# The fourth of five matrix units keeps its result in the rows of the residual, its convolution input in the tile of its left operand, and 237 vector instructions take their factor of one from a column

## The chip, the cores and the metric

One core of a Trainium2 chip runs the kernel in one launch. The metric is the device time of one execution in microseconds, the median over the runs shown. The engines of the core that matter are TensorE (PE, with its weight loads as PEld), VectorE (DVE), ScalarE (ACT), GpSimd (POOL) and SyncE (SP), whose queue issues all the transfers.

## The reference

A decoder layer over 4096 rows of 1024 numbers, all in fp32, cut to its skeleton:

```python
h = layer_norm(x)
a_val, a_gate, a_z, b_u, b_v, b_z = split(h @ w_in, 6)          # 512 columns each
a = silu(layer_norm(causal_depthwise_conv(a_val * sigmoid(a_gate), width=31)))
y_a = a * silu(a_z)
v = layer_norm(gelu(b_v)); sv = per_head_lower_triangular(w_s) @ v (chunks of 128 rows) + b_s
y_b = gelu(b_u) * sv * silu(b_z)
h = layer_norm(ALPHA * h + concat(y_a, y_b) @ w_out)             # the fourth unit, then a norm
out = h + sigmoid(h @ w_ple_gate + b) * (p @ w_ple)
```

## The kernel before

The large products are cut into five units of one shape: 4096x1024 times 1024x1024. Units 0 to 2 are three parts of `h @ w_in`, unit 3 is `w_out`, unit 4 is `w_ple_gate`. A unit has 16 steps p, each of 256 rows (two tiles j of 128). A step is one `group`, a Strassen-like scheme of seven products of 512 x 512 blocks; each product is 12 matmuls with 512 columns (a left part `ahi`, `alo` and a right part `whi`, `wlo`, three combinations, four slices of the contraction), so that a step is 84 large matmuls. The banks of the products are `pa`, `pb`, `pd`, `pe`.

Around the six points `between(i)` of a group, generators put the background work into the program: left operands of the next step, the rows' normalisation, the next unit's weights and the convolution. A scheduler then sets the order on each engine, with its own estimate of times, and gives each tile a slot of its pool. The pool `big` has seven slots of 8 KB a partition. It holds in unit 3: `hr` (the residual rows), `z` (the result), `cz` (the convolution's output and the factor silu(a_z)), `y` (the left operand), and `bq` (quarters of the weights of unit 4 on their way through four subtractions, written to `twD`). A transfer into a slot waits until the tile that held it has been read for the last time. All transfers stand in the one queue of SP, in the order of the program; one that waits holds back all behind it.

Unit 3 at step p (`body_d`): it issues the load of `hr` of p+1 (`load_h`, L706); starts `y_rows(p+2)`, which turns the convolution's output on TensorE (L679, bank `tc`), copies it to `y` on ACT (L684), takes its statistics, normalises it on ACT (L693), scales and shifts it on POOL (L695, L696), and multiplies it by silu(a_z) on POOL (L698); runs the group, whose result goes to `z`; writes in the background of the next step the normalised `z` to `zT` (`z_out`, ACT L720, transfer L721); and issues at its end the loads of p+3 (`load_y`, L664 to L671). During p = 1 to 4 the four `bq` quarters pass as well (`combos`, loads L187, direct writes L190, and four POOL subtractions, each with its write, L192 to L201).

`ss` (L91) is the helper by which VectorE combines two SBUF tiles: the low parts of weights (`wlo`, 70 of 128x1024), `v<-v,sgb` (64), `zr<-zr,c` and `zr<-zr,sg` (32 each), and 39 others, 237 instructions in all. The convolution (L388 to L399) uses the same instruction with a column of weights as its factor, on one SBUF and one PSUM input.

Of the kernel before, what the change touches and what calls it, by code (L numbers as in the profile page):

```python
# [8 lines left out]
F32 = mybir.dt.float32  # L9
# [3 lines left out]
ADD, SUB, MUL = ALU.add, ALU.subtract, ALU.mult  # L13
# [3 lines left out]
P = 128  # L17
S = 4096
D = 1024
# [3 lines left out]
C = 512  # L23
CT = C // P
# [40 lines left out]
def hybrid_layer_kernel(  # L65
# [17 lines left out]
    nc = tc.nc  # L83
    dma = nc.sync.dma_start
    act = nc.scalar.activation
    tt = nc.vector.tensor_tensor
    ptt = nc.gpsimd.tensor_tensor
    stt = nc.vector.scalar_tensor_tensor
    ID = AF.Identity

    def ss(out, a, b, op):  # L91

        return stt(out, a, 1.0, b, op0=MUL, op1=op)  # L93

    const = ctx.enter_context(tc.tile_pool(name="const", bufs=1))
    dram = ctx.enter_context(tc.tile_pool(name="dram", bufs=1, space=DRAM))
# [6 lines left out]
    def big(shape, name, dt=F32):  # L103
        return pool.tile(shape, dt, tag="big", name=name, bufs=7)
# [10 lines left out]
    def sbank(name):  # L115
        return pbank("S", name, 2)
# [4 lines left out]
    def flat(t):  # L121
        return t.rearrange("p k x -> p (k x)")
# [2 lines left out]
    make_identity(nc, ident)  # L125
    nhalf = const.tile([P, 2], F32, name="nhalf")
    nc.gpsimd.memset(nhalf, -0.5)
    cw_sb = const.tile([P, CT, W31], F32, name="cw_sb")
    cs_sb = const.tile([P, CT, NE], F32, name="cs_sb")
    cb_sb = const.tile([P, CT], F32, name="cb_sb")  # L130
# [6 lines left out]
    cD = [dram.tile([CT, P, SB // P, 2, P // 2], F32, name=f"cD{b}") for b in range(NS)]  # L137
    uD = [dram.tile([4, P, C], F32, name=f"uD{b}") for b in range(NB)]
    ybD = [dram.tile([2, P, C], F32, name=f"ybD{p}") for p in range(NP)]
    azD = [dram.tile([2, P, C], F32, name=f"azD{p}") for p in range(NP)]  # L140
    twD = [None] + [dram.tile([7, P, 4, C], F32, name=f"twD{u}") for u in range(1, 5)]

    def pair(t):
        return t.rearrange("j p d -> p j d")
# [3 lines left out]
    def moments(halves, mv):  # L148
        st = pool.tile([P, 2, 6], F32, tag="st", name="st", bufs=4)
        for i, h in enumerate(halves):  # L150
            nc.vector.bn_stats(st[:, i, :], h)
        nc.vector.bn_aggr(mv, st[:, 0 : len(halves), :])

    def mvtile(n):
        t = pool.tile([P, 2, 2], F32, tag="mv", name="mv", bufs=6)
        return t[:, 0:n, :]

    def scale_bias(mv):

        n = mv.shape[1]  # L160
        nb = pool.tile([P, 2], F32, tag="nb", name="nb", bufs=6)
        nc.vector.tensor_scalar(mv[:, :, 1], mv[:, :, 1], EPS, None, op0=ADD)  # L162
        ptt(mv[:, :, 1], mv[:, :, 1], nhalf[:, 0:n], op=ALU.pow)  # L163
        for j in range(n):
            nc.gpsimd.tensor_scalar(
                nb[:, j : j + 1], mv[:, j, 0:1], mv[:, j, 1:2], -1.0, op0=MUL, op1=MUL
            )
        return nb
# [11 lines left out]
    def combos(u):  # L180


        for c in range(4):
            q = big([P, 4, C], "bq")
            for i in range(2):
                for j in range(2):
                    dma(q[:, 2 * i + j], wq[u, i, j][:, c])  # L187
            yield
            for n, k in ((1, 0), (2, 2), (3, 3)):
                dma(twD[u][ROW[n]][:, c], q[:, k])  # L190
            ptt(q[:, 0], q[:, 1], q[:, 0], op=SUB)
            dma(twD[u][ROW[5]][:, c], q[:, 0])  # L192
            yield
            ptt(q[:, 1], q[:, 3], q[:, 1], op=SUB)
            dma(twD[u][ROW[7]][:, c], q[:, 1])
            yield
            ptt(q[:, 3], q[:, 3], q[:, 0], op=SUB)
            dma(twD[u][ROW[6]][:, c], q[:, 3])
            yield
            ptt(q[:, 2], q[:, 2], q[:, 3], op=SUB)  # L200
            dma(twD[u][ROW[4]][:, c], q[:, 2])  # L201
            yield
# [126 lines left out]
    def group(L, W, add, to12, to22, between, scale=None):  # L329


        def plus(dst, ps, i):
            if add is None:
                act(dst, ps, ID)  # L334
            elif scale is None:
                tt(dst, ps, add[i], op=ADD)
            else:
                stt(dst, add[i], scale, ps, op0=MUL, op1=ADD)

        pb = pbank("B", "pb")  # L340
        pe = pbank("E", "pe")
        product(pb, 1, L, W, True)
        product(pe, 5, L, W, True)
        pa = pbank("A", "pa")
        plus(pa, pb, 0)
        s5 = utile([P, C], "s5")
        plus(s5, pe, 3)
        between(0)
        product(pb, 6, L, W, False)
        u2 = utile([P, C], "u2")  # L350
        plus(u2, pb, 1)
        between(1)
        product(pe, 3, L, W, False)
        anchor[:] = [tt(to12, pe, u2, op=ADD)]
        between(2)
        product(pb, 7, L, W, False)
        pd = pbank("D", "pd")
        plus(pd, pb, 2)
        anchor[:] = [tt(to22, pb, s5, op=ADD)]
        between(3)  # L360
        product(pa, 2, L, W, False)
        between(4)
        product(pd, 4, L, W, False)
        between(5)
        return pa, pd
# [56 lines left out]
    def broadcast(src, n, name, tile_of=big):  # L422
        t = tile_of([P, n, src.shape[-1]], name)
        for i in range(n):
            dma(t[:, i], src[i : i + 1, :].partition_broadcast(P))
        return t
# [139 lines left out]
    for h in range(2):  # L566
        half = wsf[64 * h : 64 * (h + 1)].rearrange("p n (i m) -> p n i m", i=2)
        nc.gpsimd.affine_select(
            out=half, in_=half, pattern=[[0, NH], [1, 2], [2, 64]], compare_op=ALU.is_ge,
# [87 lines left out]
    Y, CZ, H, cgb = {}, {}, {}, []  # L657

    def load_y(p):
        b, q = p // 4, p % 4  # L660
        while (b, CT - 1) not in convolved:
            bg_conv.step(1)
        cz = big([P, 2, 2, C], "cz")
        dma(  # L664
            flat(cz[:, 0]).rearrange("p (c x) -> p c x", c=CT),
            cD[b][:, :, 2 * q : 2 * q + 2].rearrange("c p j h m -> p c (j h m)"),
        )
        dma(cz[:, 1], pair(azD[p]))
        CZ[p] = cz
        Y[p] = big([P, 2, D], "y")  # L670
        dma(Y[p][:, :, C:], pair(ybD[p]))  # L671

    def y_rows(p):
        cz, y = CZ.pop(p), Y[p]
        cc = flat(cz[:, 0]).rearrange("p (c j x) -> p c j x", c=CT, j=2)
        for j in (1, 0):
            tp = sbank("tc")
            for ct in range(CT):
                nc.tensor.transpose(  # L679
                    out=tp[:, ct * P : (ct + 1) * P],  # L680
                    in_=cc[:, ct, j],
                    identity=ident,
                )
            act(y[:, j, 0:C], tp, ID)  # L684
        yield
        mv = mvtile(2)
        for j in (1, 0):
            moments([y[:, j, 0:C]], mv[:, j, :])
        nb = scale_bias(mv)
        yield  # L690
        for j in (1, 0):
            ya = y[:, j, 0:C]
            act(ya, ya, ID, scale=mv[:, j, 1:2], bias=nb[:, j : j + 1])  # L693
            yield
            ptt(ya, ya, cgb[0][:, 0], op=MUL)  # L695
            ptt(ya, ya, cgb[1][:, 0], op=ADD)  # L696
            act(ya, ya, AF.Silu)
            ptt(ya, ya, cz[:, 1, j], op=MUL)  # L698
            yield

    def left_y(p, L):
# [2 lines left out]
    def load_h(p):  # L704
        H[p] = big([P, 2, D], "hr")
        dma(H[p], pair(hT[p]))  # L706
# [4 lines left out]
    def z_out(p, z):  # L711
        mv = mvtile(2)
        for j in range(2):
            moments([z[:, j, 0:C], z[:, j, C:]], mv[:, j, :])
            yield
        nb = scale_bias(mv)
        yield
        yield
        for j in range(2):
            act(z[:, j], z[:, j], ID, scale=mv[:, j, 1:2], bias=nb[:, j : j + 1])  # L720
            dma(zT[p][j], z[:, j])  # L721
            yield

    def body_d(p, L, W, between):
        if p == 1:
            bg_w.add(combos(4))
        h = H.pop(p)
        if p + 1 < NP:
            load_h(p + 1)
        if p + 2 < NP:  # L730
            bg_x.add(y_rows(p + 2))
        if p + 2 >= NP:
            bg_x.add(z_rows(p + 2 - NP))
        z = big([P, 2, D], "z")
        pa, pd = group(
            L, W, [h[:, 0, 0:C], h[:, 0, C:], h[:, 1, 0:C], h[:, 1, C:]],
            z[:, 0, C:], z[:, 1, C:], between, scale=ALPHA,
        )
        for j, ps in ((0, pa), (1, pd)):
            act(z[:, j, 0:C], ps, ID)  # L740
        bg_post.drain()
        bg_post.add(z_out(p, z))
        if p + 3 < NP:
            load_y(p + 3)
        elif p + 3 == NP:
            pb_.append(broadcast(prow, 2, "prow"))
            load_z(0)
        elif p + 2 == NP:
            load_z(1)
# [3 lines left out]
    def load_z(p):  # L753
        Z[p] = big([P, 2, D], "zr")
        dma(Z[p], pair(zT[p]))

    def z_rows(p):
        for j in (1, 0):
            ptt(Z[p][:, j], Z[p][:, j], pb_[0][:, 0], op=MUL)
            ptt(Z[p][:, j], Z[p][:, j], pb_[0][:, 1], op=ADD)  # L760
            yield
# [131 lines left out]
```

## Time and profile before

| | |
|---|---|
| runs | 1897.29, 1895.17, 1889.53 us; median 1895.17 |
| profiled execution | 1896.8 us, span 1895.0 us, mean granted clock 0.984 |
| instructions | 24385 |
| PE busy | 1802.0 us, 95% of the span |
| DVE, ACT, POOL busy | 1405.1, 893.4, 1270.2 us |
| HBM traffic | 211.02 MB read, 150.99 MB written |

A busy share near 95% on PE says that all that can be won lies in PE's gaps, in the stretches at a lower granted clock behind them, and in nothing else as long as PE has the same matmuls to do. Gaps show in views by stretch; the page gives means.

### The profile page before, as it was taken

What the parts mean: (1) busy time and instruction counts of PE and PEld (TensorE: products, weight loads), DVE (VectorE), ACT (ScalarE), POOL (GpSimd) and SP (SyncE); (2) the same over time, 40 slices, a digit from 0 to 9 for tenths busy, and PEclk for the clock granted to TensorE, in tenths of its full rate; (3) what the DMA queues carried; (4) which work ended last, traced back from release to release, by engine and by line L of the source; (5) the groups of instructions that cost most, each with busy time, mean ns of one, the idle gap of its engine ahead of it and who ended that gap; (6) DMA issues with size and microseconds to landing.
All of it is one profiled execution on the core that took longest, in us unless ns stands there. A gap on an engine that the chain in (4) does not pass through costs nothing.

```text
span 1895.0 us, 24385 instructions
## 1 busy us (share of the span) xinstructions
PE 1802.0 (95%) x8322; PEld 1471.8 (78%) x8322; DVE 1405.1 (74%) x2176; ACT 893.4 (47%) x1438; POOL 1270.2 (67%) x1015
## 2 busy tenths in 40 slices
PE   5799999999999999999999798999999899999999
PEld 3687788877788887788888677787887688888887
DVE  8636887797787777989889976886568756655654
ACT  4655565565455555634445544455546322332222
POOL 2878987458786676588669567776677755655541
PEclk9899999999999999999999998999999999999999
DMA  6579776586734444899666856755446322222211
GB/s 240 193 233 352 254 231 214 182 297 210 239 112 148 138 160 150 304 353 328 211 200 222 308 192 228 250 186 191 168 167 236 119 101 78 89 90 95 100 55 52
DMA packets 184940, 363.62 MB, mean 192 GB/s; under 512 B 49648, under 2 KB 74224, under 8 KB 177136
## 3 DMA queue, kind: packets, MB, share of 16 engines
q1 hardware_dynamic: 184816, 362.07, 55.4%
q8 instruction: 66, 1.08, 0.2%
q14 instruction: 58, 0.48, 0.1%
HBM read 211.02 MB, written 150.99 MB: 191 GB/s over the span
## 4 chain that ended last, share of the span: by engine, by line
PE 75%; DVE 10%; DMA 7%; ACT 3%; issue 3%; POOL 2%; SPq 0%; DVEq 0%; POOLq 0%; ACTq 0%
PE pb L316 9%; PE pb L317 9%; PE pb L318 9%; PE pe L318 6%; PE pe L316 6%; PE pe L317 6%; PE pp L809 5%; PE tp L261 3%; PE pd L316 3%; PE pd L317 3%; PE pd L318 3%; PE pa L316 3%; PE pa L317 3%; PE pa L318 3%; DVE wlo L93 2%
## 5 line engine op out<-in xcount | busy, mean ns | idle before, releaser
L236 POOL TENSOR_TENSOR alo<-s,ahi 128x512 fp32r<-128x512 f32 x192 | 266.7, 1402 | 275.5 <-ACT ahi L235 271.6
L316 PE MATMUL pb<-whi,ahi 128*128 128x512 f32 x960 | 386.8, 403 | 13.2 <-ACT pa L334 5.4
L317 PE MATMUL pb<-wlo,ahi 128*128 128x512 f32 x960 | 379.3, 395 | 1.9 <-DVE wlo L93 1.9
L318 PE MATMUL pb<-whi,alo 128*128 128x512 f32 x960 | 379.0, 395 | 0.1
L316 PE MATMUL pe<-whi,ahi 128*128 128x512 f32 x640 | 257.0, 402 | 16.8 <-ACT ahi L235 7.5
L317 PE MATMUL pe<-wlo,ahi 128*128 128x512 f32 x640 | 253.3, 396 | 4.2 <-DVE wlo L93 4.0
L318 PE MATMUL pe<-whi,alo 128*128 128x512 f32 x640 | 255.5, 399 | 1.6 <-POOL alo L236 1.5
L316 PEld LDWEIGHTS pb<-whi,ahi 128*128 128x128 f32 x960 | 183.1, 191 | 57.0 <-ACT pa L334 9.0
L318 PEld LDWEIGHTS pb<-whi,alo 128*128 128x128 f32 x960 | 182.7, 190 | 40.0 <-POOL alo L236 0.5
L317 PEld LDWEIGHTS pb<-wlo,ahi 128*128 128x128 f32 x960 | 183.2, 191 | 38.8 <-DVE wlo L93 2.9
L236 POOL TENSOR_TENSOR alo<-qa,ahi 128x512 fp32r<-128x512 f32 x128 | 171.5, 1355 | 44.9 <-ACT ahi L235 44.8
L390 DVE SCALAR_TENSOR_TENSOR acc<-ca,cs_sb,acc 128x512 f32<-128x512 f32 x240 | 180.0, 750 | 4.1
L235 ACT ACTIVATE ahi<-s 128x512 fp32r<-128x512 f32 x192 | 119.9, 629 | 131.6 <-DVE s L288 49.7
L399 DVE SCALAR_TENSOR_TENSOR acc<-ca,cw_sb,acc 128x512 f32<-128x512 f32 x240 | 179.1, 746 | 0.8 <-POOL ca L383 0.6
L396 DVE SCALAR_TENSOR_TENSOR acc<-zy,cw_sb,acc 128x512 f32<-128x512 f32 x224 | 167.0, 746 | 2.6 <-POOL zy L382 1.5
L316 PEld LDWEIGHTS pe<-whi,ahi 128*128 128x128 f32 x640 | 121.8, 190 | 42.2 <-ACT ahi L235 8.7
L236 POOL TENSOR_TENSOR alo<-qb,ahi 128x512 fp32r<-128x512 f32 x96 | 126.9, 1328 | 39.6 <-ACT ahi L235 38.8
L317 PEld LDWEIGHTS pe<-wlo,ahi 128*128 128x128 f32 x640 | 121.7, 190 | 30.3 <-DVE wlo L93 6.5
L236 DVE TENSOR_TENSOR alo<-tp,ahi 128x512 fp32r<-128x512 f32 x144 | 97.9, 684 | 62.1 <-ACT ahi L235 60.0
L318 PEld LDWEIGHTS pe<-whi,alo 128*128 128x128 f32 x640 | 121.7, 190 | 26.8 <-POOL alo L236 2.5
L316 PE MATMUL pd<-whi,ahi 128*128 128x512 f32 x320 | 129.9, 406 | 5.5 <-ACT pd L334 3.8
L163 POOL TENSOR_TENSOR mv<-mv,nhalf 128x2 f32<-128x2 f32 (+1 forms) x81 | 55.4, 690 | 108.6 <-DVE mv L162 108.0
(147 smaller groups left out, 3994.7 us busy)
## 6 DMA issues: line engine op xcount, KB each, us to landing
qa<-qD SPq DMA_DIRECT2D x32, 1024.0 KB, 6.2
twD<-bq SPq DMA_DIRECT2D x112, 256.0 KB, 5.8
wst<-twD SPq DMA_DIRECT2D x28, 1024.0 KB, 7.2
qb<-qD SPq DMA_DIRECT2D x32, 768.0 KB, 6.5
xr<-in_x SPq DMA_DIRECT2D x32, 512.0 KB, 5.6
hT<-xr SPq DMA_DIRECT2D x32, 512.0 KB, 3.8
qD<-s SPq DMA_DIRECT2D x64, 256.0 KB, 2.9
bq<-in_wq SPq DMA_DIRECT2D x64, 256.0 KB, 5.0
```

The costliest lines, as they stand in the source:

```text
L93: return stt(out, a, 1.0, b, op0=MUL, op1=op)
L163: ptt(mv[:, :, 1], mv[:, :, 1], nhalf[:, 0:n], op=ALU.pow)
L235: act(hi, src, ID)
L236: eng.tensor_tensor(lo, src, hi.bitcast(F32), op=SUB)
L261: nc.tensor.transpose(out=tp[:, kk * P : (kk + 1) * P], in_=rows[:, j, k * P : (k + 1) * P], identity=ident,)
L316: nc.tensor.matmul(ps, lhsT=ah[:, k, :], rhs=wh[:, k, :], start=start and k == 0, stop=False, **kw)
L317: nc.tensor.matmul(ps, lhsT=ah[:, k, :], rhs=wl[:, k, :], start=False, stop=False, **kw)
L318: nc.tensor.matmul(ps, lhsT=al[:, k, :], rhs=wh[:, k, :], start=False, stop=k == 3, **kw)
L390: stt(even, src, w, even, op0=MUL, op1=ADD)
L396: stt(dst, src, cw_sb[:, ct, 2 * k + 1 : 2 * k + 2], odd if k else even, op0=MUL, op1=ADD)
L399: stt(src if k == NE - 1 else even, src, cw_sb[:, ct, 2 * k : 2 * k + 1], even, op0=MUL, op1=ADD,)
L809: nc.tensor.matmul(pp, lhsT=l[:, k, ts], rhs=r[:, k, cs], start=k == 0 and l is ph and r is wp_hi, stop=k == 1 and l is pl,)
```

## The change

It has two parts. In unit 3 the result is written over the residual rows (`z = h`), and the convolution's output is loaded into the left half of `y`, in two transfers of 256 KB with pieces of 512 bytes where there was one of 512 KB with pieces of 1 KB; TensorE turns it out of `y` and ACT writes it back to the same place. `cz` then holds silu(a_z) alone, at half its size. A step so takes three slots of `big` (`hr`, `y`, `cz`) where it took four. In `ss`, the factor 1.0 is read from a column of ones in SBUF, and one POOL instruction fills this column.

```diff
     def ss(out, a, b, op):
-        return stt(out, a, 1.0, b, op0=MUL, op1=op)
+        return stt(out, a, one, b, op0=MUL, op1=op)
...
+    one = const.tile([P, 1], F32, name="one")
+    nc.gpsimd.memset(one, 1.0)
...
-        cz = big([P, 2, 2, C], "cz")
-        dma(
-            flat(cz[:, 0]).rearrange("p (c x) -> p c x", c=CT),
-            cD[b][:, :, 2 * q : 2 * q + 2].rearrange("c p j h m -> p c (j h m)"),
-        )
-        dma(cz[:, 1], pair(azD[p]))
-        CZ[p] = cz
         Y[p] = big([P, 2, D], "y")
+        for j in (1, 0):
+            dma(
+                Y[p][:, j, 0:C].rearrange("p (c x) -> p c x", c=CT),
+                cD[b][:, :, 2 * q + j].rearrange("c p h m -> p c (h m)"),
+            )
+        CZ[p] = big([P, 2, C], "cz")
+        dma(CZ[p], pair(azD[p]))
         dma(Y[p][:, :, C:], pair(ybD[p]))
...
-        cc = flat(cz[:, 0]).rearrange("p (c j x) -> p c j x", c=CT, j=2)
...
-                    in_=cc[:, ct, j],
+                    in_=y[:, j, ct * P : (ct + 1) * P],
...
-            ptt(ya, ya, cz[:, 1, j], op=MUL)
+            ptt(ya, ya, cz[:, j], op=MUL)
...
-        z = big([P, 2, D], "z")
+        z = h
```

The change also lets the scheduler order anew. On SP's queue, this is the stretch around the loads for step 4 of unit 3 (`cz_10539` before, `y_10543` after; `bq_10363` and `bq_10532` before, `bq_10367` and `bq_10536` after, are the first and second quarter; `z_10091` before and `hr_10086` after hold the result of step 0). Before:

```order
L201 DMA twD4_176<-bq_10363 128x512
L721 DMA zT0_93<-z_10091 128x1024
L187 DMA bq_10532<-in_wq 128x512
L721 DMA zT0_93<-z_10091 128x1024
L187 DMA bq_10532<-in_wq 128x512 x3
L190 DMA twD4_176<-bq_10532 128x512
L664 DMA cz_10539<-cD1_130 128x4x256
L668 DMA cz_10539<-azD4_161 128x2x512
L190 DMA twD4_176<-bq_10532 128x512
```

After:

```order
L203 DMA twD4_178<-bq_10367 128x512
L189 DMA bq_10536<-in_wq 128x512 x4
L192 DMA twD4_178<-bq_10536 128x512
L722 DMA zT0_95<-hr_10086 128x1024
L192 DMA twD4_178<-bq_10536 128x512
L722 DMA zT0_95<-hr_10086 128x1024
L192 DMA twD4_178<-bq_10536 128x512
L194 DMA twD4_178<-bq_10536 128x512
L667 DMA y_10543<-cD1_132 128x4x128 x2
```

The two writes of the result now stand behind the second quarter's loads and its first write, and the load for step 4 stands behind one write of `twD` that follows a POOL subtraction. In the slots, `y_10543` lies where `hr_10086` lay, so its load waits for both writes of `zT0`; `cz_10539` waited for them too.

The same queue around the loads for step 5 (`z_10299` before and `hr_10094` after hold the result of step 1; `bq_10762` and `bq_10766` are the third quarter). Before:

```order
L190 DMA twD4_176<-bq_10762 128x512
L721 DMA zT1_94<-z_10299 128x1024
L190 DMA twD4_176<-bq_10762 128x512 x2
L721 DMA zT1_94<-z_10299 128x1024
L664 DMA cz_10786<-cD1_130 128x4x256
L668 DMA cz_10786<-azD5_162 128x2x512
L192 DMA twD4_176<-bq_10762 128x512
L671 DMA y_10789<-ybD5_146 128x2x512
L706 DMA hr_10791<-hT4_81 128x2x1024
L195 DMA twD4_176<-bq_10762 128x512
```

After:

```order
L192 DMA twD4_178<-bq_10766 128x512 x3
L722 DMA zT1_96<-hr_10094 128x1024
L194 DMA twD4_178<-bq_10766 128x512
L722 DMA zT1_96<-hr_10094 128x1024
L197 DMA twD4_178<-bq_10766 128x512
L667 DMA y_10790<-cD1_132 128x4x128 x2
L672 DMA cz_10793<-azD5_164 128x2x512
L673 DMA y_10790<-ybD5_148 128x2x512
L200 DMA twD4_178<-bq_10766 128x512
```

The load for step 5 moved behind the writes of the first two POOL subtractions of the quarter (L194, L197), which stood behind it before (L192, L195). Its slot was that of a left operand (`y_10295`) and is now that of `hr_10094`, so it waits for `zT1` to be written, which it did not do before.

## Rows read from the trace of the kernel before

**Rows 1.** The page, busy time of each engine.

```profile
PE 1802.0 (95%) x8322; PEld 1471.8 (78%) x8322; DVE 1405.1 (74%) x2176; ACT 893.4 (47%) x1438; POOL 1270.2 (67%) x1015
```

**Rows 2.** The page, the chain that ended last, by engine.

```profile
PE 75%; DVE 10%; DMA 7%; ACT 3%; issue 3%; POOL 2%; SPq 0%; DVEq 0%; POOLq 0%; ACTq 0%
```

**Rows 3.** Windows: start and boundary to unit 4; length, PE, PEld, DVE, ACT, POOL, clock, DMA.

```profile
0.00:73.00 73.00, 38.39 (x130) 27.60 (x131) 62.61 (x83) 38.62 (x50) 32.44 (x31) 0.88 0.62 222
...
1456.00:1519.00 63.00, 54.41 (x231) 43.34 (x230) 48.82 (x53) 28.88 (x41) 45.10 (x24) 0.92 0.44 157
```

**Rows 4.** Windows, the first five steps of unit 3, same columns.

```profile
1078.00:1110.60 32.60, 24.30 (x111) 19.81 (x110) 26.45 (x36) 14.81 (x23) 20.59 (x17) 0.84 0.70 228
1110.60:1132.70 22.10, 21.76 (x106) 17.66 (x105) 18.55 (x35) 10.74 (x17) 16.79 (x19) 1.00 0.53 187
1132.70:1161.00 28.30, 25.35 (x114) 20.53 (x113) 16.77 (x32) 11.64 (x19) 17.36 (x18) 0.88 0.67 239
1161.00:1188.60 27.60, 23.57 (x109) 19.24 (x108) 20.32 (x39) 11.02 (x17) 22.83 (x23) 0.94 0.68 226
1188.60:1212.40 23.80, 22.36 (x109) 18.07 (x108) 18.26 (x35) 12.01 (x20) 18.34 (x20) 1.00 0.87 308
```

**Rows 5.** Waits ahead of the tile `tc`: releaser, us in all, times.

```profile
  DMA cz<-cD: 10.9, 6
  DVE alo L236: 6.4, 1
```

**Rows 6.** Timeline of PE in unit 3: start, us each, idle before and releaser.

```profile
1089.89 1.09 PE L679 MATMUL tc<-ident,cz 128*128 128x128 f32 x4 [6.37 <-DVE alo L236]
...
1139.45 1.09 PE L679 MATMUL tc<-ident,cz 128*128 128x128 f32 x4 [2.95 <-DMA cz<-cD]
...
1141.19 0.63 PE L318 MATMUL pb<-whi,alo 128*128 128x512 f32 x1
...
1168.34 1.11 PE L679 MATMUL tc<-ident,cz 128*128 128x128 f32 x8 [4.03 <-DMA cz<-cD]
```

**Rows 7.** Timeline of SP's queue before steps 4 and 5: start and length of an issue.

```profile
1127.93 0.41 SPq L721 DMA_DIRECT2D zT<-z  x1
...
1131.17 0.33 SPq L190 DMA_DIRECT2D twD<-bq  x1
1132.42 0.38 SPq L664 DMA_DIRECT2D cz<-cD  x1
...
1134.80 0.33 SPq L190 DMA_DIRECT2D twD<-bq  x1
...
1160.31 0.71 SPq L721 DMA_DIRECT2D zT<-z  x1
1161.11 1.10 SPq L664 DMA_DIRECT2D cz<-cD  x1
...
1168.61 0.33 SPq L195 DMA_DIRECT2D twD<-bq  x1
```

**Rows 8.** The page, transfers: count, KB each, median us from issue to landing.

```profile
zT<-z SPq DMA_DIRECT2D x32, 512.0 KB, 2.9
...
cz<-cD SPq DMA_DIRECT2D x16, 512.0 KB, 4.3
...
pf<-in_pT SPq DMA_DIRECT2D x16, 256.0 KB, 2.6
```

**Rows 9.** VectorE's groups by form: count | busy us, mean ns.

```profile
L390 DVE SCALAR_TENSOR_TENSOR acc<-ca,cs_sb,acc 128x512 f32<-128x512 f32 x240 | 180.0, 750 | 4.1
...
L93 DVE SCALAR_TENSOR_TENSOR wlo<-wst,whi 128x1024 fp32r<-128x1024 f32 x70 | 106.9, 1544 | 7.2 <-ACT whi L176 6.3 <-PE pb L318 0.8
...
L93 DVE SCALAR_TENSOR_TENSOR zr<-zr,c 128x512 f32<-128x512 f32 x32 | 43.9, 1373 | 1.0
...
L338 DVE SCALAR_TENSOR_TENSOR pa<-hr,pb 128x512 f32<-128x512 f32 x16 | 11.1, 694 | 13.1 <-PE pb L318 13.1
```

**Rows 10.** Instructions of line 93: count, ns min/median/max, first and last start.

```profile
L93 DVE SCALAR_TENSOR_TENSOR wlo<-wst,whi x70: 1164/1218/3379, 13.7 to 1475.4; 128x1024 fp32r<-128x1024 f32 x70
```

## The prediction

> **What bounds the kernel now.** I began with the busy times. PE is busy for 95% of the span [rows 1], and the chain that ended last lies on PE for 75%, on DVE for 10% and on transfers for 7% [rows 2]. The change takes no matmul away, so what it can win is PE's idle time and the time that PE runs at its lower clock. The windows show where these are. The first 73 us hold 34.6 us of idle time (73.00 - 38.39), and the passage to unit 4 holds 8.6 us in 63 [rows 3]. The rest that concerns the change lies in the first steps of unit 3: an undisturbed step takes 22.10 us at a clock of 1.00, and the first, third, fourth and fifth of these windows take 32.60, 28.30, 27.60 and 23.80 us [rows 4]. That is 10.5 + 6.2 + 5.5 + 1.7 = 23.9 us more. This stage is what the first part of the change works on.
>
> Next I asked what ends the idle time there. Ahead of the transposes into `tc`, PE waits 10.9 us for the load of the convolution's output and 6.4 us for `alo` on DVE [rows 5]. The timeline gives the single waits: 6.37 us in the first window, for DVE; 2.95 us in the third and 4.03 us in the fourth, both for the load [rows 6]. After each such gap a 512-column matmul takes 0.63 us [rows 6], and the window's granted clock falls to 0.84, 0.88 and 0.94 [rows 4]: parts of these windows run at 1.2 GHz, not 2.4. PE's busy time shows what this costs: 24.30, 25.35 and 23.57 us against 21.76, so 2.5, 3.6 and 1.8 us [rows 4].
>
> **The first gap.** The 6.37 us of the first window end with `alo` on DVE [rows 6]. DVE reaches it late, behind the split of the weights, and its order there hardly differs after the change. The transposed data are not what is late. I take 0 us for it, and its 10.5 us stay.
>
> **The loads for steps 4 and 5.** One fewer tile for each step should let loads go out earlier, but the slots and the queue decide. For step 4, PE was ready at 1139.45 - 2.95 = 1136.5. The load was issued at 1132.42 and its data came at 1139.45 [rows 6, 7], so it took 7.0 us, though the median for this kind of load is 4.3 [rows 8]. After the change the load still waits for both writes of the result of step 0, which now stand behind the second quarter's loads and its direct writes. The bounds: if the second write of `zT` still goes out at 1127.93 [rows 7], it lands 2.9 us later, at 1130.8, and a 256 KB load needs 2.6 us (the row of `pf`) [rows 8]; its data are there at 1133.4 and there is no wait. If this write goes out behind the quarter's second direct write, at 1134.80 + 0.33 [rows 7], it lands at 1138.0, and the load comes 2.6 to 4.3 us behind, at 1140.6 to 1142.3: a wait of 4.1 to 5.8 us. The quarter's loads no longer stand behind a write of `zT` that waits for ACT, so its chain starts earlier than before; I take the middle of the outer ends, 1137.9, a wait of 1.4 us, and 1.5 us less than before.
>
> For step 5, PE was ready at 1168.34 - 4.03 = 1164.3, the load was issued at 1161.11 and took 7.2 us [rows 6, 7]. Its new slot makes it wait for the result of step 1 to be written: with the second write issued at 1160.31 as before [rows 7] plus 2.9 us, the load goes out at 1163.2, later than before. But it now comes in halves of 256 KB, of which PE needs only the first to begin. It lands 2.6 to 4.3 us later, at 1165.8 to 1167.5, a wait of 1.5 to 3.2 us. The late end is the queue: the load stands behind the write of the quarter's second subtraction, which went out at 1168.61 before [rows 7]. If it does so again, the data come at 1171.5 to 1173.2, a wait of 7.2 to 8.9 us. On POOL the two subtractions now stand ahead of the left operands' subtractions that delayed them, so the early end is nearer. I take 1167, a wait of 2.7 us, and 1.3 us less.
>
> From step 6 on I take 0 us for the loads: only 1.7 us are to be had at one step, and thereafter the loads have a step in hand. The two shorter gaps take about half of one and a third of the other's time at the lower clock with them: 3.6 x 1.5 / 2.95 + 1.8 x 1.3 / 4.03 = 2.4 us, of which I count 1.5, since how long the clock stays low need not follow the length of the gap. The first part then gives -1.5 - 1.3 - 1.5 = -4.3 us. The 16 more transfers cost SP some 0.4 us each (the issue at 1132.42 took 0.38 [rows 7]), spread over 16 steps of 22 us. Writing the transposed values back into `y` adds no instruction.
>
> **The column of ones.** All 237 instructions of `ss` change their form. The trace has no instruction with two SBUF inputs and a column as factor. The nearest row is the convolution's: 750 ns with a column, on one SBUF and one PSUM input, against 694 ns for the same kind with a constant factor [rows 9]. So I take 56 ns more, and 237 x 0.056 = 13.3 us of DVE. Of DVE's 1405.1 busy us, the chain holds 10% of 1895.0, or 189.5 us, which is 13.5% [rows 1, 2]. By this share the path gets 1.8 us. The ends are 0 (all hidden behind PE) and 13.3 us (all on the path).
>
> Could the column make them faster? The splits `wlo` have a median of 1218 ns, a mean of 1544 and a maximum of 3379 [rows 10, 9], and `zr<-zr,c` has a mean of 1373 where the alone-standing form takes about 694 [rows 9]. The long ones lie beside POOL instructions. The Trainium skill, SBUF — State Buffer, "Who interferes with whom", says that a DVE instruction with two SBUF inputs contends with a GpSimd instruction that reads SBUF; the trace agrees (1373 ns against 694). Nothing in that rule depends on where the scalar comes from, and by "Scalar operands" of DVE: scalar operands, raw-bit mode, write accounting and state across instructions, a column takes up no second tensor stream; the second input of these instructions is still a tensor, so by both the stretch stays as it is. I take no gain here.
>
> **The order anew.** At the start and at the passage to unit 4 the scheduler puts DVE's splits and PE's pieces in a slightly other order. This work decides PE's idle 34.6 and 8.6 us [rows 3]. I take 0, with the 8.6 us of the passage as a bound to either side.
>
> **Sum.** 1896.8 - 4.3 + 1.8 = 1894.3 us. The profiled execution lies 1.6 us above the median of the runs, whose ends are 8 us apart; 0.5%, or 9.5 us, is about what a measurement of this kernel can tell from no change. I predict 1894 us.
>
> **Rivals.**
> - *The loads come early.* One fewer slot for each step puts all the waits for the convolution's output aside: 10.9 us [rows 5] and the 3.6 + 1.8 us of low clock, 16.3 in all, less 1.8 for the column: 1882 us. For it: seven slots for three tiles a step. Against it: slots that the writes of `zT` free late.
> - *The column frees DVE from GpSimd.* The stretched part of the two costliest groups goes: 70 x (1544 - 1218) ns = 22.8 us and 32 x (1373 - 694) ns = 21.7 us, 44.5 us of DVE [rows 9, 10], 13.5% of it on the path, 6.0 us. With it the backlog ahead of `alo` in unit 3 (6.4 + 2.5 us) and about half the passage's 8.6 us: 19 us together, so 1877 us. For it: the convolution's instructions with a column have a mean of 750 ns beside the same POOL. Against it: these have only one SBUF tensor.
> - *The loads come later (slower).* Both loads take their late ends, since the writes of a quarter of weights stand ahead of them: the waits become about 5.0 and 8.0 us instead of 2.95 and 4.03, +6.0, and the low clock grows with them by 3.6 x 2.1 / 2.95 + 1.8 x 4.0 / 4.03 = 4.3; with the column's 1.8, +12 and 1909 us. It decides from the point at which the write of the second subtraction for step 5 goes out after 1165 on before's clock.
> - *The form with a column reads its two tensors in turn.* Then each takes twice its 694 ns, 237 x 0.694 = 164 us of DVE and 13.5% of it on the path: 1919 us. Nothing in the trace speaks for it or shows that it is not so.
>
> **Chances.** Little change as summed: 0.47, its own range 1887 to 1903. Loads early: 0.15. Column frees DVE: 0.10. Loads later: 0.14. Tensors in turn: 0.03. Order anew beyond the bound: 0.06 faster, 0.05 slower. So faster 0.31, same 0.47, slower 0.22. From 1876 to 1910 the range takes in the first rival, most of the second and half or more of the third, and leaves out less than 2 in 10.
>
> **What would show it.** In unit 3 the waits of PE ahead of `tc` at steps 4 and 5 should be 1 to 3 us each, ended by the load into `y`, and the one of about 6 us behind `alo` should stand. The `v<-v,sgb` and `wlo` instructions should read some 50 ns longer where alone, and as stretched as before beside POOL. Wrong would be: medians of `zr<-zr,c` at 700 to 750 ns (the second rival); no waits for loads in unit 3 and a clock of 1.00 from the third window on (the first); waits of 5 us and more at steps 4 and 5 with `twD` writes ahead on SP's queue (the third); or a start longer or shorter by more than 9 us, which is the order alone.

## The result

The changed kernel is slower: 1911.31 us (median of 4 runs, 1908.88 to 1915.45) against 1896.23 us for the kernel before (4 runs, 1889.53 to 1898.48). The ratio is 1.0089, with a 95% interval from 1.0071 to 1.0107, that is 15 us or 0.9%. The forecast was 1894 us, from 1876 to 1910, with the largest chance on no change.

| us | before | changed |
|---|---|---|
| span of the profiled execution | 1895.0 | 1907.6 |
| PE busy | 1802.0 | 1805.4 |
| DVE busy | 1405.1 | 1420.7 |
| to the second step of unit 0 | 73.4 | 78.2 |
| from there to the first step of unit 3 | 1004.6 | 1003.9 |
| first five steps of unit 3 | 134.3 | 129.7 |
| its further ten steps | 221.6 | 221.9 |
| last step of unit 3 and six of unit 4 | 192.9 | 205.2 |
| the rest | 268.2 | 268.7 |

The stretches are taken between the first matmuls into `pb` of the steps. Two pieces lose, 4.8 us at the start and 12.3 us at the passage to unit 4; one gains, 4.6 us in the first steps of unit 3. The page of the changed kernel, busy time and then the chain by engine, answers to [rows 1, 2]:

```profile
PE 1805.4 (95%) x8322; PEld 1472.7 (77%) x8322; DVE 1420.7 (74%) x2176; ACT 893.7 (47%) x1438; POOL 1262.8 (66%) x1016
...
PE 76%; DVE 11%; DMA 5%; POOL 4%; issue 3%; ACT 1%; SPq 0%; POOLq 0%; DVEq 0%; ACTq 0%
```

DVE holds 15.6 us more, transfers have a smaller share of the chain, DVE and POOL a larger one. The windows of the changed kernel, for the start, the five steps, and 63 us from the first step of unit 4 (columns as in [rows 3, 4]):

```profile
0.00:73.00 73.00, 33.85 (x109) 23.57 (x110) 60.45 (x74) 35.17 (x44) 28.06 (x30) 0.86 0.57 202
1082.10:1114.00 31.90, 23.60 (x100) 18.75 (x101) 25.34 (x33) 15.01 (x24) 19.37 (x15) 0.84 0.64 214
1114.00:1136.60 22.60, 21.18 (x105) 17.16 (x104) 19.25 (x37) 9.74 (x16) 16.50 (x19) 1.00 0.62 215
1136.60:1159.70 23.10, 22.29 (x110) 18.10 (x109) 17.79 (x34) 10.20 (x16) 14.66 (x16) 1.00 0.77 260
1159.70:1186.00 26.30, 23.02 (x109) 17.95 (x108) 19.59 (x35) 12.66 (x20) 24.75 (x24) 1.00 0.76 261
1186.00:1211.90 25.90, 24.35 (x120) 19.99 (x119) 21.39 (x39) 10.71 (x17) 21.83 (x22) 1.00 0.84 269
1460.60:1523.60 63.00, 53.20 (x226) 41.72 (x225) 50.38 (x55) 27.11 (x39) 39.36 (x21) 0.92 0.38 132
```

The third of the five steps fell from 28.30 to 23.10 us and its clock rose from 0.88 to 1.00; the fourth fell by 1.3 us, its clock also at 1.00; the fifth grew by 2.1 us. The first, which waits for DVE, is nearly as long as before. The waits of PE in the changed kernel (releaser, us in all, times, longest):

```profile
PE tp L263 <- DVE xr L93: 22.2, 4, 11.4
...
PE pb L318 <- ACT pa L336: 8.1, 6, 3.9
PE pb L318 <- DVE pa L338: 7.1, 2, 3.6
...
PE pe L320 <- POOL alo L238: 3.9, 3, 3.1
...
PE tc L680 <- DMA y<-cD: 1.6, 1, 1.6
```

The same waits for `pa` in the kernel before:

```profile
PE pb L316 <- ACT pa L334: 5.4, 8, 1.5
...
PE pb L316 <- DVE pa L336: 2.4, 1, 2.4
```

The wait for the convolution's output, 10.9 us in [rows 5], is down to 1.6 us, and waits on the other engines have grown. One of them is in the fourth of these steps: PE waits 3.06 us for `alo` on POOL, where it had waited 4.03 us for the load.

```profile
1166.43 0.50 PE L320 MATMUL pe<-whi,alo 128*128 128x512 f32 x1 [3.06 <-POOL alo L238]
```

The instructions with the column in the changed kernel (count, ns min/median/max, first and last start; [rows 10] has the first of them before):

```profile
L93 DVE SCALAR_TENSOR_TENSOR wlo<-wst,one,whi x70: 1224/1274/3372, 13.7 to 1472.7; 128x1024 fp32r<-128x1024 f32 x70
...
L93 DVE SCALAR_TENSOR_TENSOR zr<-zr,one,c x32: 750/1254/1905, 1496.8 to 1898.4; 128x512 f32<-128x512 f32 x32
L93 DVE SCALAR_TENSOR_TENSOR zr<-zr,one,sg x32: 750/752/2158, 1508.7 to 1904.0; 128x512 f32<-128x512 f32 x32
```

They are 56 ns longer in the median of the splits (1218 to 1274), and the long ones beside POOL are still there. A split is the subtraction that makes the low part `wlo` of a weight.

### The profile page after: what moved, and what is told of

Its sections match the earlier page's. It is cut to its first block, busy times and chain, and to the rows that moved or that the text cites. A ratio compares the mean times of both kernels' runs of the same rounds, so it can differ in the third digit from the quotient of the medians.

```text
span 1907.6 us, 24493 instructions
## 1 busy us (share of the span) xinstructions
PE 1805.4 (95%) x8322; PEld 1472.7 (77%) x8322; DVE 1420.7 (74%) x2176; ACT 893.7 (47%) x1438; POOL 1262.8 (66%) x1016
## 4 chain that ended last, share of the span: by engine, by line
PE 76%; DVE 11%; DMA 5%; POOL 4%; issue 3%; ACT 1%; SPq 0%; POOLq 0%; DVEq 0%; ACTq 0%
PE pb L318 9%; PE pb L320 9%; PE pb L319 9%; PE pe L318 6%; PE pe L320 6%; PE pe L319 6%; PE pp L810 4%; PE tp L263 3%; PE pd L318 3%; DVE wlo L93 3%; PE pa L318 3%; PE pa L319 3%; PE pd L319 3%; PE pd L320 3%; PE pa L320 3%
## 5 line engine op out<-in xcount | busy, mean ns | idle before, releaser
L238 POOL TENSOR_TENSOR alo<-s,ahi 128x512 fp32r<-128x512 f32 x192 | 261.0, 1370 | 278.4 <-ACT ahi L237 267.0
L320 PE MATMUL pa<-whi,alo 128*128 128x512 f32 x320 | 127.8, 400 | 2.5 <-DVE alo L238 2.5
```

The source lines that it names most:

```text
L238: eng.tensor_tensor(lo, src, hi.bitcast(F32), op=SUB)
L320: nc.tensor.matmul(ps, lhsT=al[:, k, :], rhs=wh[:, k, :], start=False, stop=k == 3, **kw)
```

## The experiments

All were timed in five rounds against the kernel before on the same chip. The medians of before were 1891.12, 1892.96 and 1893.82 us in the three sets, so the ratios are compared, not the medians. Each ratio stands with its 95% interval.

**The column alone, the first part alone, and the halves of the first part.** The edits to the kernel before, in this order: the column; both edits of unit 3; the shared result; the load into `y`.

```diff
-        return stt(out, a, 1.0, b, op0=MUL, op1=op)
+        return stt(out, a, one, b, op0=MUL, op1=op)      # e1
...
-        z = big([P, 2, D], "z")
+        z = h                                            # e2, e3
...
+                Y[p][:, j, 0:C].rearrange("p (c x) -> p c x", c=CT),
+                cD[b][:, :, 2 * q + j].rearrange("c p h m -> p c (h m)"),   # e2, e4
...
```

> The kernel before with the column of ones alone. Theory A (the column is the loss: some 60 ns more for each of 237 instructions, at the start and the unit boundaries on the path, and an order made for it): +8 to +15 us, start about 5 us longer, the passage to unit 4 about 8 us longer. Theory B (the slots of the first part are the loss, at the passage to unit 4): 0 to +5 us, from the start alone. Theory C (each build gets its own order, and losses at the boundaries are its chance): anything from -5 to +15, not additive with the next run.

> The changed kernel with the constant 1.0 in place of the column, so the first part of the change alone. Theory A: faster than before by 4 to 9 us, since the waits for loads in steps 4 and 5 of unit 3 are gone. Theory B: slower by 5 to 10 us, with the loss at the passage to unit 4 still there. Theory C: not the difference of the changed kernel and the run with the column alone; its own sum of boundary waits.

> The kernel before with the result written over the residual rows alone (convolution output still loaded into cz). Theory A: -2 to -6 us: a slot more is free, the loads for steps 4 and 5 come earlier. Theory B: if this part is the loss at the passage to unit 4, +5 to +10 us. If the loads come no earlier, 0.

> The kernel before with the convolution output loaded into y in two halves and turned in place alone (result still in its own tile). Theory A: 0 to -4 us: the first half lands sooner, cz is half as large but holds a slot as before. Theory B: 0, if the loss needs the slot that the shared result frees.

Measured: the column alone 1.0083 (1.0070 to 1.0095); the first part alone 1.0015 (1.0006 to 1.0023); the shared result alone 1.0023 (1.0010 to 1.0037); the load into `y` alone 1.0054 (1.0042 to 1.0066). By the total, the column alone costs nearly what both parts cost, as theory A said. The places do not agree: theory A's 8 us at the passage to unit 4 are not in e1, whose seven steps there take 191.0 us where the kernel before takes 192.9 and the changed kernel 205.2. Nor did theory A's gain of 4 to 9 us from the first part come: it costs 0.15%. The gains that were expected of its halves did not come either. The load into `y` alone costs more than both halves together, so the halves do not add up.

**Which of the two, the longer instructions or the order?** With the column, the scheduler made another order: of 2176 instructions on DVE 314 have to be moved to turn the order of before into that of e1, of 8322 on PE 1633. It is the column as a factor that does this; the one memset alone moves nothing (e5 has it, with the order of before on PE, DVE and ACT). In the next three runs the factor is exchanged after the order is set, so that order, slots and waits are kept; a fourth, e8, leaves the factor out (edits shortened):

```diff
     with _tile.TileContext(nc, schedule_with_timeline_sim=True) as tc:
         hybrid_layer_kernel(tc, *args)
+    for i in ss_instructions:                            # order and waits are set by now
+        replace(i, ins=[i.ins[0], column, i.ins[2]])     # e5: order of before
+        replace(i, ins=[i.ins[0], 1.0, i.ins[2]])        # e6: order made for e1; e7: of the changed kernel
...
-        return stt(out, a, 1.0, b, op0=MUL, op1=op)
+        return tt(out, a, b, op=op)                      # e8: no factor at all, same order as before
```

> The order, slots and waits of the kernel before; only after the order is set, the constant 1.0 of the 237 instructions is exchanged for the column. Theory D (the loss of the column lies in the longer instructions): +10 to +16 us, as with the column and its own order. Theory E (it lies in the order that the scheduler makes when the factor is a column): +1 to +4 us, which is 237 times 60 ns by the share of VectorE that lies on the path.

> The order, slots and waits that the scheduler makes for the column alone, with the constant 1.0 put back after the order is set. Theory D: -2 to +3 us against before. Theory E: +10 to +14 us, with the start still some 4 us longer, since the order of the start is kept.

> The order, slots and waits of the changed kernel, with the constant 1.0 put back after the order is set. Theory D: about the time of the first part alone, +2 us against before. Theory E: +10 to +14 us, 1 to 4 us less than the changed kernel.

> The kernel before with the 237 instructions as plain two-tensor operations without a factor, in the same order on every engine. All theories: 0 us, instructions as long as with the constant (about 690 ns where alone), and as stretched beside GpSimd; a difference of more than 3 us would say that the form decides how VectorE and GpSimd share.

Measured: the column in the order of before 1.0028 (1.0013 to 1.0042); the constant in the column's order 1.0051 (1.0036 to 1.0066); the constant in the changed kernel's order 1.0076 (1.0062 to 1.0090); no factor 1.0003 (0.9992 to 1.0014). The first two add to 0.79%, and the column with its own order gave 0.83%. So about a third of the column's loss, 5.3 us, is the longer instructions, and two thirds, 9.7 us, the order. Theory E is right in its direction, with numbers a little off: the instructions cost more than 1 to 4 us, the order in e6 slightly less than 10. The changed kernel's order, in which the first part's slots and loads are included, costs 0.76% even with the constant. In this order the instructions make up only 0.13%, the difference to the 0.89% of the changed kernel (the two intervals overlap), so their price seems to hang on the order too.

The control e8 has the durations of the constant. Its splits (ns min/median/max), and then the same rows of e8 and of e5, the column in the order of before (count | busy us, mean ns):

```profile
L93 DVE TENSOR_TENSOR wlo<-wst,whi x70: 1185/1219/3372, 13.3 to 1471.2; 128x1024 fp32r<-128x1024 f32 x70
```

```profile
L93 DVE TENSOR_TENSOR zr<-zr,c 128x512 f32<-128x512 f32 x32 | 45.1, 1408 | 1.0
```

```profile
L93 DVE SCALAR_TENSOR_TENSOR zr<-zr,one,c 128x512 f32<-128x512 f32 x32 | 50.1, 1565 | 1.1
```

With the factor in a column, without a factor, or with a constant, the instructions with two tensors in SBUF are stretched beside POOL, to means of 1565, 1408, and 1373 ns in [rows 9]; the convolution's, with one, have 750. In all three traces every `zr<-zr,c` that is over 10% longer than where alone overlaps a POOL instruction. The form does not decide how VectorE and GpSimd share. The Trainium skill, SBUF — State Buffer, "Who interferes with whom", names two SBUF inputs as the condition, and these rows agree with it.

The order can be read at the start. DVE in the kernel before:

```profile
54.39 1.21 DVE L93 SCALAR_TENSOR_TENSOR wlo<-wst,whi 128x1024 fp32r<-128x1024 f32 x1
55.53 3.36 DVE L93 SCALAR_TENSOR_TENSOR xr<-xr,eb 128x1024 f32<-128x1024 f32 x1
58.81 3.38 DVE L93 SCALAR_TENSOR_TENSOR wlo<-wst,whi 128x1024 fp32r<-128x1024 f32 x1
```

DVE in e6, the constant in the column's order:

```profile
53.18 2.35 DVE L93 SCALAR_TENSOR_TENSOR xr<-xr,eb 128x1024 f32<-128x1024 f32 x2
55.45 3.36 DVE L93 SCALAR_TENSOR_TENSOR wlo<-wst,whi 128x1024 fp32r<-128x1024 f32 x1
58.74 3.35 DVE L93 SCALAR_TENSOR_TENSOR xr<-xr,eb 128x1024 f32<-128x1024 f32 x1
```

And PE at this place, the kernel before and then e6:

```profile
59.04 2.94 PE L261 MATMUL tp<-ident,xr 128*128 128x128 f32 x12 [9.43 <-DVE xr L93]
```

```profile
62.24 2.94 PE L265 MATMUL tp<-ident,xr 128*128 128x128 f32 x12 [12.69 <-DVE xr L93]
```

The same two instructions have changed places. Both are stretched to 3.4 us beside POOL. The last half of the rows `xr`, for which PE waits, now stands behind a split of weights for which nobody waits yet. PE goes on at 62.24 instead of 59.04 us. This is one place of several: the profile of e6 also has 2.4 us more than before in unit 1 and 2.3 us more in the further ten steps of unit 3.

**The column at the start or behind it.** `begun` is empty until the first step is put into the program.

```diff
-        return stt(out, a, 1.0, b, op0=MUL, op1=op)
+        return stt(out, a, 1.0 if begun else one, b, op0=MUL, op1=op)   # e9
+        return stt(out, a, one if begun else 1.0, b, op0=MUL, op1=op)   # e10
```

> The kernel before with the column in the instructions of the start alone (the first weights and the first two tiles of rows, ahead of the first step), the constant elsewhere; the start then has the order of the kernel with the column alone, in which one split of weights stands ahead of the last half of the rows that TensorE waits for. If the start is where a third of the column's loss comes from: the second step begins 4 to 5 us later than before, and the time is +4 to +6 us. If that loss is made up later on: 0.

> The column in all instructions behind the start, the constant at the start, whose order is then that of the kernel before. If the order at the start is a third of the loss: start as before, +9 to +11 us in all, the rest from units 1 and 3 and from the passages. If the start is the whole loss: 0 to +3.

Measured: the column at the start alone 1.0031 (1.0019 to 1.0043), and the second step of unit 0 begins 5.0 us later than before in the profile. The column behind the start alone 1.0021 (1.0009 to 1.0034), with the second step where it was before. So the column in the 34 instructions of the start costs 5.9 us, of which 5.0 show at the start, and nothing makes them up later. The order behind the start differs from before as well (842 of 8188 instructions on PE have to be moved), so not all of it need come from the start. The column in the other 203 gives 4 us where 9 to 11 were expected. The two add to 0.52%, not 0.83%: the order behind the start differs from that of e1, and so do its losses.

**The passage to unit 4.** In the first part alone, the profile shows shorter steps in unit 3 and a longer passage. The five steps of e2:

```profile
1072.60:1105.00 32.40, 25.04 (x110) 19.96 (x109) 25.88 (x35) 13.63 (x21) 19.65 (x16) 0.84 0.64 212
1105.00:1124.70 19.70, 19.36 (x95) 15.80 (x94) 16.58 (x32) 9.64 (x15) 13.88 (x15) 1.00 0.65 225
1124.70:1150.40 25.70, 22.38 (x110) 18.06 (x109) 17.64 (x34) 12.11 (x19) 18.56 (x19) 1.00 0.76 260
1150.40:1176.10 25.70, 22.99 (x109) 17.83 (x108) 19.11 (x36) 11.18 (x18) 21.80 (x22) 1.00 0.80 276
1176.10:1199.80 23.70, 22.55 (x109) 17.84 (x107) 20.01 (x36) 11.42 (x18) 21.52 (x22) 1.00 0.79 245
```

They sum to 127.2 us where [rows 4] sum to 134.4, so 7.2 us less. From the last step of unit 3 on, the same seven steps as in the table above take 198.8 us instead of 192.9. PE waits there for sums on DVE, in e2:

```profile
1457.48 0.47 PE L316 MATMUL pb<-whi,ahi 128*128 128x512 f32 x1 [3.40 <-DVE pa L336]
1465.85 1.12 PE L261 MATMUL tp<-ident,zr 128*128 128x128 f32 x4 [2.89 <-DVE alo L236]
```

and DVE is busy with splits of unit 4's weights, four in a row between the sum `pa` and the part `alo` that PE needs, the two pairs at 3.44 and 4.46 us beside POOL, where a pair takes 2.34 alone:

```profile
1456.66 0.68 DVE L336 TENSOR_TENSOR pa<-pb,gb 128x512 f32<-128x512 f32 x1
1457.25 3.44 DVE L93 SCALAR_TENSOR_TENSOR wlo<-wst,whi 128x1024 fp32r<-128x1024 f32 x2
...
1460.73 4.46 DVE L93 SCALAR_TENSOR_TENSOR wlo<-wst,whi 128x1024 fp32r<-128x1024 f32 x2
1465.12 0.68 DVE L236 TENSOR_TENSOR alo<-tp,ahi 128x512 fp32r<-128x512 f32 x1
```

Two runs, made from the first part alone, keep a result tile of its own in the last steps, so that the slots at the passage are used as before:

```diff
-        z = h
+        z = h if p < NP - 2 else big([P, 2, D], "z")     # e11; NP - 3 in e12
```

> The first part alone (constant kept), with a result tile of its own in the last two of the 16 steps of unit 3. If the shared result loses at the passage to unit 4 by letting the new weights in early, so that their splits stand in VectorE's queue ahead of the first sums of unit 4: the passage takes 5 to 8 us less than in the run of the first part alone, and the time is 4 to 7 us below the kernel before. If the loss has another cause: as the first part alone, +2.

> As the run before, with a result tile of its own in the last three steps. If the slots at the passage decide, again 4 to 7 us below the kernel before. If each build's order at the passage is a matter of chance, one of these two gains and the other does not.

Measured: 1.0034 (1.0021 to 1.0047) for the last two, 1.0000 (0.9990 to 1.0009) for the last three. The seven steps at the passage take 201.3 us in e11 and 196.0 us in e12, against 198.8 in e2. So the theory as put, that giving the slots back brings 5 to 8 us there, falls: of two edits that do it, one loses 2.5 us and the other gains 2.8. That the shared slots have a part is not excluded: the orders in which the result shares the rows to the end (the changed kernel, e2 and e3) all have these four splits in a row and 198.8 us or more at the passage. What makes a good order there stays open. No run was faster than the kernel before.

**By stages.** One profile of each build, us; builds with the same order stand together.

| build | to the second step of unit 0 | first five steps of unit 3 | seven steps at the passage |
|---|---|---|---|
| before: constant | 73.4 | 134.3 | 192.9 |
| its order, no factor (e8) | 74.6 | 133.0 | 192.5 |
| its order, column (e5) | 74.7 | 131.8 | 196.7 |
| column alone (e1) | 78.2 | 135.4 | 191.0 |
| its order, constant (e6) | 76.4 | 135.4 | 191.8 |
| changed kernel | 78.2 | 129.7 | 205.2 |
| its order, constant (e7) | 76.4 | 130.0 | 202.6 |
| first part alone (e2) | 72.9 | 127.2 | 198.8 |
| shared result alone (e3) | 72.8 | 126.4 | 200.3 |
| load into `y` alone (e4) | 73.3 | 135.9 | 195.3 |
| column at the start (e9) | 78.4 | 126.2 | 195.4 |
| column behind it (e10) | 73.4 | 137.2 | 192.7 |
| own result, last two (e11) | 72.8 | 129.8 | 201.3 |
| own result, last three (e12) | 73.5 | 127.7 | 196.0 |

Builds with the same order differ by up to 4.2 us in a stage, builds with different orders by up to 14. The changed kernel loses most at the passage, where the column's own order loses nothing. And the five steps of unit 3 are shortest in e9, whose code for unit 3 is that of the kernel before: the order alone moves this stage as far as the first part does.

## Why the prediction was wrong

**The step that failed** is "The order anew": "I take 0, with the 8.6 us of the passage as a bound to either side." The column's order alone costs 0.51%, 9.7 us (e6), and the changed kernel's order, with the first part's slots and loads in it, 0.76%, 14.4 us (e7). With the factor in a column the scheduler made another order throughout the program, not at two places: 1833 of 8322 instructions on PE and 455 of 2176 on DVE have to be moved to turn the order of before into that of the changed kernel. I gave a loss beyond the bound a chance of 0.05, but set no rival for it. My sign for it, a start longer by more than 9 us, did not show: the start is 4.8 us longer, and the passage loses 12.3.

**The first gap** stayed, as said: the first step of unit 3 takes 31.9 us in the changed kernel and 32.4 in e2, at a clock of 0.84 both times. Its waits are others, though: in the changed kernel PE waits 3.61 us for ACT's copy into `y` and 4.67 us for `alo`, instead of 1.93 us for the load and 6.37 for `alo`.

**The loads for steps 4 and 5.** A gain of 4.3 us was predicted, and the five steps gained 4.6 us in the changed kernel and 7.2 in e2. The size was right for the changed kernel, but by luck, since the mechanism was in the main another. The queue of SP in the changed kernel, answering to [rows 7], and the turns on PE (the transposes into `tc`) for steps 4 and 5, answering to [rows 6]:

```profile
1133.46 0.43 SPq L722 DMA_DIRECT2D zT<-hr  x1
...
1134.80 0.73 SPq L722 DMA_DIRECT2D zT<-hr  x1
...
1139.18 0.92 SPq L667 DMA_DIRECT2D y<-cD  x2
...
1161.88 0.39 SPq L722 DMA_DIRECT2D zT<-hr  x1
1165.18 0.32 SPq L197 DMA_DIRECT2D twD<-bq  x1
1165.61 1.00 SPq L667 DMA_DIRECT2D y<-cD  x2
```

```profile
1142.26 0.63 PE L680 MATMUL tc<-ident,y 128*128 128x128 f32 x4
...
1169.01 0.63 PE L680 MATMUL tc<-ident,y 128*128 128x128 f32 x4
```

Neither turn shows a wait, where 1 to 3 us each were predicted. Yet the loads did not all come earlier. Step 4's load was issued 4.4 us behind the second write of `zT`; its first half landed 5.5 us into the third of the five steps, where the whole load of before had landed 6.6 us into it. Step 5's stood behind the write of the second subtraction, as feared in the third rival, and its first half landed 9.2 us into the fourth step, 2 us later than the load before (7.2). What took the waits away is mainly the order on PE: 22 large matmuls now stand ahead of the turns in each of the two steps, where 14 stood before, some 1.8 us of work more. At step 5 PE was also held by `alo` on POOL for 3.06 us in the meantime, a wait that I had not priced; two of POOL's subtractions for the weights now stand ahead of it, where one stood. The halves help little: the second landed 0.7 and 1.1 us behind the first, the halves alone (e4) gain nothing in these steps, while the shared result alone (e3) gains 7.9 us, and e9, with neither, 8.1.

**The column.** The 56 ns for each instruction were right (1218 to 1274 ns). In the order of before the path got 5.3 us of it (e5, 0.13% to 0.42%), not 1.8, so the term was mis-sized threefold, inside its bounds of 0 to 13.3; in the changed kernel's order it is 0.13%, about 2.5 us. DVE's share of the chain is too low a price where PE waits for DVE. At the start DVE is busy for 62.6 of 73 us [rows 3]. There the second step begins at 78.2 us with the column (e1 and the changed kernel) and at 76.4 with the constant in the same orders (e6, e7): 1.8 us, where 34 instructions of 56 to 60 ns make some 2.0. In e5's profile no single place holds the 5.3 us; the largest piece is 3.8 us at the passage.

**The rivals.** Two signs of the first rival nearly came, one load wait of 1.6 us and a clock of 1.00 from the third step on, but through the order on PE, and the five steps gained 4.6 us, which were given back at the passage. The column did not free DVE (e5, e8), nor did it read its tensors in turn (752 ns where alone, not 1388). The waits of 5 us and more of the third rival did not come. The right case, the order, was the one without a mechanism.

**The sum as measured**: 0.28% for the instructions, 0.51% for the column's order, 0.15% for the first part with its order make 0.94%; the changed kernel has 0.89%. That these agree is in part luck: the three were measured in three different orders, and the changed kernel loses most at a place where the column alone loses nothing.

## What to carry to other kernels

Where a scheduler sets the order by estimated times, an edit that makes it order anew is an edit of the whole program; price the order by running the edit with the order held, in both directions, before blaming the instruction. Where an engine sets the end of a stretch, a longer instruction can count nearly whole, as at this start, whatever the engine's share over the span. A wait that is gone does not show that its load came earlier: see when the load landed and what work now stands ahead. And it counts only if no other queue is late in its place, so follow the gain through the next passage.

## What was not expected of the hardware

A column as the scalar factor costs the same 56 to 60 ns on an instruction of 512 elements (693 to 752 ns for `zr<-zr,sg`) as on one of 1024 (1218 to 1274 ns), so at these two sizes it does not grow with the elements. A constant factor costs nothing: the splits have a median of 1218 ns with it and 1219 ns without a factor (e8).
